# RWKV: the solve by three products on the right-hand side, and values mixed in rows of tokens

## The chip, the cores and the metric

The kernel runs on one core of a Trainium2 chip. The time is the device time of one execution in microseconds (us), from the first to the last instruction on the core. In the text PE is the engine that multiplies matrices (TensorE), DVE the vector engine, ACT the activation engine (ScalarE), POOL the GpSimd engine, and SP the engine that issues nearly all transfers.

## The reference, cut to what matters

The model has two blocks on 256 tokens of width 2048; all is in float32. The change lies in the second block, in a group of 16 RWKV heads of 64 channels. For each token the projection p is mixed with that of the token before it, and a recurrence runs over the tokens:

```
prev = jnp.pad(p, ((0, 0), (1, 0), (0, 0)))[:, :-1]
p = p + (prev - p) * mu
r, k, v, xw, xa, xg = split_cols_2(p, RWKV_SPLITS)
...
def step(state, inp):
    r_t, w_t, k_t, v_t, kk_t, a_t = inp
    sa = jnp.einsum('bhvk,bhk->bhv', state, -kk_t)
    state = (state * w_t[:, :, None, :]
             + sa[..., None] * (kk_t * a_t)[:, :, None, :]
             + v_t[..., None] * k_t[:, :, None, :])
    return state, jnp.einsum('bhvk,bhk->bhv', state, r_t)
```

The kernel doesn't run the recurrence token by token. It takes the tokens in two blocks of 128. Within a block the removed part sa of each token depends on those of the tokens before it, which is a triangular system with a unit diagonal, 128 by 128 for each head: (I - N) x = rhs, with N strictly triangular.

## The kernel before

Each projection is a product in three parts (a high and a low part of each factor: lines 163 to 165). The weights arrive by transfers of 512 KB that SP issues (line 159), ACT rounds them to the high part wh (line 148), and DVE forms the low part wl (lines 151 and 154). PE accumulates in acc.

The 16 heads are worked in two halves of 8 (`rwkv_half`, hf = 0 and 1), and a half in two groups of 4 heads (`heads4`, hg = 0 and 1), which are generators run step by step in turn (`together`). A half begins with the projections of k, r and v (`rwkv_in`). The function `project` calls `evac` for each block of tokens, which scales acc into a tile pn with the tokens on the partitions (line 1226); `shifted` transposes pn, so that channels lie on the partitions and tokens in columns, and `shift` mixes each column with the one before it: one activation and one instruction on DVE for each 128 channels (lines 1210 and 1211). For v (the tile rv) the result is transposed back by `rows` to the tile vn, tokens on the partitions, with 8 transposes and two copies (lines 1367 and 1368).

Then come the decay (pd at line 1280, the scan cs at line 1288), the norm of the keys, whose square root is taken by Newton steps on DVE (lines 1312 to 1319: nv, nt, ni), and the matrices sa of both groups and both token blocks (line 1391). The diagonal blocks of 32 by 32 of all 16 systems of the half are inverted together on DVE (lines 1411 and 1412), transposed to invt and invx (lines 1417 and 1418), and `spread` puts them into block-diagonal matrices of 128 by 128, four heads to an instruction (line 1433).

In `heads4` the inverse of the whole system is then formed by doubling the block size twice (l = 5 and 6): pz is the product of the matrix with the inverse so far, zt keeps the part of the level (line 1453), and pw is added to the inverse wt (line 1458). Between the levels wt is transposed to xt by PE and ACT (lines 1445 and 1447). Then pk is formed from v (line 1462), copied to rhs, and pg is the inverse times rhs (line 1471). For the first block (t = 0) rhs has 64 columns for each head, for the second 128. After that come the scores psr, the outputs py, the state pst and, at the end of the half, the norm of the outputs and a gate (the product pgt).

Each engine carries out its instructions in order. The framework sets that order when the kernel is built: it moves the instructions of an engine against each other by its own estimate of when they can start. Projections that belong to later work (`feed`) are laid between the steps of the attention and of half 0. In half 1's solve hardly any are left.

Of the kernel before, what the change touches and what calls it, by code (L numbers as in the profile page):

```python
# [12 lines left out]
AL = mybir.AluOpType  # L13
# [41 lines left out]
def tile_kernel(ctx: ExitStack, tc: tile.TileContext, I: dict, out: bass.AP):  # L55
# [27 lines left out]
    def tl(tag, shape=None, dt=F, name=None):  # L83
        pool, (n, bufs) = (sb, BASE[tag]) if tag in BASE else (phase[1], phase[2][tag])
        shape = [128, n] if shape is None else shape
        return pool.tile(shape, dt, name=name or tag, tag=tag, bufs=bufs)
# [1116 lines left out]
    G.memset(seg2, 1.0)  # L1203
    G.memset(seg2.rearrange("p (n c) -> p n c", c=128)[:, :, 0:1], 0.0)
    strict = cst[:, C_LT:C_LT + 128]
    upto = cst[:, C_LE:C_LE + 128]
# [13 lines left out]
    def shifted(c0, name, nt, dt_, tr, feed=None, early=0):  # L1220
# [14 lines left out]
        return dst  # L1235

    CDEC = math.exp(-0.5)
    yr = []
# [23 lines left out]
    def rwkv_in(hf, feed):  # L1262
        how = ("f", "xt", bgT) if hf else ("m", "g", lambda nat, q: transpose2(lambda t, kt: nat[t][:, kt * 128:(kt + 1) * 128], q))
        kx = shifted(1024 + hf * 512, "rk", *how, feed=feed, early=0 if hf else 2)
        if hf == 0:
            ranks()
        return kx, shifted(hf * 512, "rr", *how), shifted(2048 + hf * 512, "rv", *how)

    def rwkv_half(hf, kx, rx, vx):
        c8 = slice(hf * 4, hf * 4 + 4)  # L1270
# [90 lines left out]

        vn = tl("g", [128, 2, 512], name="vn")

        def rows(dst, x, t):
            p = pside([128, 4, 128], name="prow")
            for q in range(4):
                PE.transpose(p[:, q], x[:, q, t * 128:(t + 1) * 128], ident)
            S.copy(dst, flat(p))

        for t in range(2):  # L1370
            rows(vn[:, t], vx, t)
        kn = tl("l", name="kn")
# [49 lines left out]
        def heads4(hg):  # L1422
            s0 = None
            for t in range(2):
# [12 lines left out]

                wt = spread(invt, "wt")
                xt = spread(invx, "xt")
                for l in range(5, 7):  # L1440
                    yield
                    if l == 6:
                        px = pside([128, 4, 128], name="px")
                        for i in range(4):
                            PE.transpose(px[:, i], wt[:, i], ident)
                        xt = tl("m", [128, 4, 128], name="xt")
                        S.copy(xt, px)
                        yield
                    pz = pside([128, 4, 128], name="pz")
                    for i in range(4):  # L1450
                        PE.matmul(pz[:, i], nt_(i), xt[:, i], start=True, stop=True)  # L1451
                    zt = tl("m", [128, 4, 128], name="zt")
                    V.tensor_tensor(zt, pz, bc4(lev[:, l * 128:(l + 1) * 128]), op=AL.mult)
                    yield
                    pw = pside([128, 4, 128], name="pw")
                    for i in range(4):
                        PE.matmul(pw[:, i], zt[:, i], wt[:, i], start=True, stop=True)  # L1457
                    V.tensor_tensor(wt, pw, wt, op=AL.add)
                yield
# [6 lines left out]
                if t:  # L1466
                    G.tensor_copy(rhs[:, :, 64:], an[:, hv].rearrange("p (h k) -> p h k", h=4))
                yield
                pg = pside([128, 4, 128], name="pg")
                for i in range(4):  # L1470
                    PE.matmul(pg[:, i, :n], wt[:, i], rhs[:, i, :n], start=True, stop=True)
                ga = tl("m", [128, 4, 128], name="ga")
# [440 lines left out]
```

## Time and profile before

| | us |
|---|---|
| three runs | 2555.61, 2565.97, 2565.65 (median 2565.65) |
| profiled execution, its own time | 2557.92 |
| its span in the trace | 2556.2 |
| PE busy | 2422.8 (95%) |
| DVE busy | 1796.2 (70%) |
| ACT busy | 1170.2 (46%) |
| POOL busy | 172.1 (7%) |

The times of the three runs and of the profiled execution differ by 10 us. Starts in the trace are counted from the beginning of the span. In a timeline row the figure in brackets is how long the engine stood idle before the instruction, and what ended it. An f32 product shows as two instructions of PE, so a row of 8 heads reads x16. The granted clock of PE was 0.984 of full speed over the span.

### The profile page before, as it was taken

Reading aid. Unit: us, or ns where it says so; the run is one execution under the profiler, and the core shown is the slowest. Engines: PE = TensorE matmul, PEld = TensorE weight load, DVE = VectorE, ACT = ScalarE, POOL = GpSimd, SP = SyncE. Lnnn points to the kernel's source line nnn. Section 1 sums busy time; section 2 is a strip of 40 time slices with the busy share of each in tenths; the row PEclk is TensorE's granted clock in tenths of the full one; section 3 lists DMA queues with packets and bytes.
Section 4 is the critical chain, followed back from the end, with each engine's and each line's share of the span. In section 5 each row is a group of like instructions: output and inputs, shape, how many; then the busy total and the mean of one; then the engine's idle time right before and its main releaser. Section 6 shows DMA issues by size and latency. Waiting matters only on the chain.

```text
span 2556.2 us, 32427 instructions
## 1 busy us (share of the span) xinstructions
PE 2422.8 (95%) x11491; PEld 1928.6 (75%) x11491; DVE 1796.2 (70%) x2991; ACT 1170.2 (46%) x1560; POOL 172.1 (7%) x169
## 2 busy tenths in 40 slices
PE   8999998889989998998999999999999999999998
PEld 5667766778767776787878677787888888888886
DVE  5898657997897888967687978755655544555544
ACT  6543244444653544445642452445544433444433
POOL 0000010220230010002020120100000000000000
PEclk9999999999999999999999999999999999999999
DMA  7877547676656788755633243145466555666554
GB/s 262 276 251 225 170 153 242 218 232 228 198 183 218 233 282 288 259 182 158 198 94 110 80 136 99 63 163 192 133 189 182 186 187 187 189 184 187 201 188 154
DMA packets 267358, 483.11 MB, mean 189 GB/s; under 512 B 21137, under 2 KB 45547, under 8 KB 267195
## 3 DMA queue, kind: packets, MB, share of 16 engines
q1 hardware_dynamic: 266875, 480.60, 58.4%
q8 instruction: 90, 1.47, 0.2%
q14 instruction: 73, 0.60, 0.1%
q10 hardware_dynamic: 320, 0.44, 0.1%
HBM read 477.82 MB, written 3.15 MB: 188 GB/s over the span
## 4 chain that ended last, share of the span: by engine, by line
PE 61%; DVE 18%; DMA 11%; issue 6%; ACT 3%; POOL 1%; SPq 0%; DVEq 0%; ACTq 0%; POOLq 0%
PE acc L165 17%; PE acc L164 17%; PE acc L163 17%; DMA ar<-in_w_ada 8%; DVE wl L154 6%; DVE aa L405 3%; PE trp L236 2%; ACT wh L148 1%; DMA lnb<-in_ln_b 1%; PE pw L1457 1%; PE pz L1451 1%; DVE u L1411 1%; DVE inv L1412 1%; DMA wr<-in_w_in_e 1%; DMA wr<-in_w_in_o 0%
## 5 line engine op out<-in xcount | busy, mean ns | idle before, releaser
L148 ACT CAST wh<-wr 128x1024 fp32r<-128x1024 f32 (+2 forms) x736 | 760.3, 1038 | 991.6 <-PE acc L165 804.6
L164 PE MATMUL acc<-wl,xh 128*128 128x512 f32 (+2 forms) x2560 | 1005.5, 393 | 22.9 <-DVE wl L154 22.7
L163 PE MATMUL acc<-wh,xh 128*128 128x512 f32 (+2 forms) x2560 | 1011.8, 396 | 14.1 <-ACT xh L253 6.1
L165 PE MATMUL acc<-wh,xl 128*128 128x512 f32 (+2 forms) x2560 | 1003.5, 393 | 2.4 <-DVE xl L254 1.9
L154 DVE TENSOR_TENSOR wl<-wr,wh 128x512 fp32r<-128x512 f32 (+2 forms) x928 | 622.3, 702 | 176.8 <-ACT wh L148 176.1
L164 PEld LDWEIGHTS acc<-wl,xh 128*128 128x128 f32 x2560 | 485.1, 189 | 135.8 <-DVE wl L154 37.2
L151 DVE TENSOR_TENSOR wl<-wr,wh 128x1024 fp32r<-128x1024 f32 x272 | 333.3, 1225 | 357.4 <-ACT wh L148 355.4
L163 PEld LDWEIGHTS acc<-wh,xh 128*128 128x128 f32 x2560 | 484.6, 189 | 127.1 <-ACT wh L148 10.0
L165 PEld LDWEIGHTS acc<-wh,xl 128*128 128x128 f32 x2560 | 484.8, 189 | 106.3 <-issue 4.0
L405 DVE SCALAR_TENSOR_TENSOR aa<-ar,cs,aa 128x512 f32<-128x512 f32 x240 | 191.0, 796 | 72.8 <-DMA ar<-in_w_ada 71.5
L165 PE MATMUL acc<-wh,ucl 128*128 128x512 f32 x128 | 50.9, 398 | 0.0
L164 PE MATMUL acc<-wl,uch 128*128 128x512 f32 x128 | 50.7, 396 | 0.0
L163 PE MATMUL acc<-wh,uch 128*128 128x512 f32 x128 | 49.8, 389 | 0.0
L381 DVE SCALAR_TENSOR_TENSOR am<-ar,cs,am 128x512 f32<-128x512 f32 x60 | 42.6, 746 | 7.3 <-DMA ar<-in_w_ada 7.3
L722 PE MATMUL pp<-eq,ek 128*128 128x128 f32 x224 | 29.4, 286 | 6.1 <-DVE ek L734 6.1
L722 PEld LDWEIGHTS pp<-eq,ek 128*128 128x128 f32 x224 | 28.5, 201 | 8.4 <-issue 5.0
L1055 POOL TENSOR_TENSOR sgo<-sgo,psc 128x512 f32<-128x512 f32 x8 | 14.6, 1850 | 295.5 <-ACT sgo L1049 164.8
L350 PE MATMUL ada<-wl,c 128*4 128x512 f32 x64 | 26.0, 406 | 4.2 <-DVE wl L154 4.2
L164 PE MATMUL acc<-wl,dh 128*128 128x512 f32 x64 | 26.2, 410 | 3.8 <-DVE wl L154 3.7
L457 DVE SCALAR_TENSOR_TENSOR xl<-trp,pr,xh 128x256 fp32r<-128x256 f32 x48 | 22.3, 480 | 10.1 <-ACT xh L456 9.9
L1866 ACT ACTIVATE un<-acc,rml 128x512 f32<-128x512 f32 x32 | 22.0, 689 | 15.6 <-PE acc L165 15.6
L163 PEld LDWEIGHTS acc<-wh,uch 128*128 128x128 f32 x128 | 24.4, 191 | 5.6
(592 smaller groups left out, 2457.3 us busy)
## 6 DMA issues: line engine op xcount, KB each, us to landing
ar<-in_w_ada SPq DMA_DIRECT2D x288, 256.0 KB
wr<-in_w_in_e SPq DMA_DIRECT2D x128, 512.0 KB
wr<-in_w_up SPq DMA_DIRECT2D x128, 512.0 KB
wr<-in_w_down SPq DMA_DIRECT2D x128, 512.0 KB
wr<-in_w_in SPq DMA_DIRECT2D x80, 512.0 KB
wr<-in_w_in_o SPq DMA_DIRECT2D x64, 512.0 KB
wr<-in_w_ada SPq DMA_DIRECT2D x64, 256.0 KB
wr<-in_w_out_e SPq DMA_DIRECT2D x32, 512.0 KB
```

The lines of the kernel that those rows point to most:

```text
L148: S.copy(wh, wr)
L151: engines[0].tensor_tensor(wl, wr, wh.bitcast(F), op=AL.subtract)
L154: engines[q % 2].tensor_tensor(wl[:, q], wr[:, q], wh[:, q].bitcast(F), op=AL.subtract)
L163: PE.matmul(acc, xh, wh, start=start, stop=False)
L164: PE.matmul(acc, xh, wl, start=False, stop=False)
L165: PE.matmul(acc, xl, wh, start=False, stop=stop)
L236: PE.transpose(pt[:, q, t * 128:(t + 1) * 128], src(t, kt + q), ident)
L350: PE.matmul(acc, c4[:, k0 + q], wl[:, q], start=False, stop=k0 + q == 15)
L381: V.scalar_tensor_tensor(acc[a], w[:, q], col, acc[a], op0=AL.mult, op1=AL.add)
L405: V.scalar_tensor_tensor(acc, w, cs[:, k:k + 1], acc, op0=AL.mult, op1=AL.add)
L722: PE.matmul(pp[:, h, t], kx[:, 2 * h + c, s * 128:(s + 1) * 128], qx[:, 2 * h + c, t * 128:(t + 1) * 128], start=c == 0, stop=c == 1)
L1411: V.tensor_tensor(u, inv[:, j + 1:, j:j + 1].to_broadcast([128, n, j]), inv[:, j:j + 1, :j].to_broadcast([128, n, j]), op=AL.mult)
```

## The change

There are two edits. First, v is no longer transposed, mixed in columns and transposed back. A new function, `shifted_rows`, leaves v in rows of tokens: ACT scales acc into pn as before, a transfer issued from ACT's queue copies the rows 0 to 126 of pn into the rows 1 to 127 of a second tile pv, another brings the last row of the first block into the first row of the second, and for the first block the first row is cleared by POOL. The mixing constants arrive as a broadcast (mur, 512 columns). DVE then forms vn in three instructions for each block of tokens: pv - pn, times mur, plus pn.

Second, the inverse of the 128 by 128 system is not formed. With D the block-diagonal inverse (spread to dt and dx) and M the part of the product of N with D outside the diagonal blocks (pmm, masked by the new constant off32 into mt), the solution is D times a sum of powers of M on rhs. There are four diagonal blocks, so the sum ends with the third power: x = rhs, then three times x = M x + rhs (px, and x on DVE), and pg is D times x.

```
--- before.py
+++ after.py
@@ -1202,6 +1202,8 @@
     seg2 = tl("c", name="seg2")
     G.memset(seg2, 1.0)
     G.memset(seg2.rearrange("p (n c) -> p n c", c=128)[:, :, 0:1], 0.0)
+    off32 = pconst([128, 128], "off32")
+    V.tensor_scalar(off32, cst[:, C_BD32:C_BD32 + 128], -1.0, 1.0, op0=AL.mult, op1=AL.add)
     strict = cst[:, C_LT:C_LT + 128]
     upto = cst[:, C_LE:C_LE + 128]
     bc4 = lambda m: m[:, None, :].to_broadcast([128, 4, 128])
@@ -1232,6 +1234,29 @@
             for r in range(2):
                 k = c0 // 128 + q + r
                 shift(dst[:, q + r], pt[:, r], pr3[:, MU + k:MU + k + 1], omu[:, k:k + 1])
+        return dst
+
+    def shifted_rows(c0, name, nt, dt_):
+
+        nat, prev = {}, {}
+        mu = bcast("bc", I["rwkv_mu_2"][0, c0:c0 + 512], 512, name="mur")
+
+        def evac(cb, t, acc):
+            nat[t] = tl(nt, name="pn")
+            prev[t] = tl(nt, name="pv")
+            S.activation(nat[t], acc, AF.Identity, scale=rs1[t])
+            nc.scalar.dma_start(prev[t][1:], nat[t][:127])
+            if t:
+                nc.scalar.dma_start(prev[t][:1], nat[0][127:])
+            else:
+                G.memset(prev[t][:1], 0.0)
+
+        project(hT, w2, c0, 512, evac, lead=0)
+        dst = tl(dt_, [128, 2, 512], name=name)
+        for t in range(2):
+            V.tensor_tensor(prev[t], prev[t], nat[t], op=AL.subtract)
+            V.tensor_tensor(prev[t], prev[t], mu, op=AL.mult)
+            V.tensor_tensor(dst[:, t], prev[t], nat[t], op=AL.add)
         return dst
 
     CDEC = math.exp(-0.5)
@@ -1264,9 +1289,9 @@
         kx = shifted(1024 + hf * 512, "rk", *how, feed=feed, early=0 if hf else 2)
         if hf == 0:
             ranks()
-        return kx, shifted(hf * 512, "rr", *how), shifted(2048 + hf * 512, "rv", *how)
-
-    def rwkv_half(hf, kx, rx, vx):
+        return kx, shifted(hf * 512, "rr", *how), shifted_rows(2048 + hf * 512, "vn", *how[:2])
+
+    def rwkv_half(hf, kx, rx, vn):
         c8 = slice(hf * 4, hf * 4 + 4)
         wup = tl("m", name="wup")
         nc.sync.dma_start(wup[:64], I["w_decay_up_2"][0][:, hf * 512:(hf + 1) * 512])
@@ -1359,16 +1384,12 @@
             S.activation(e, e, AF.Exp, scale=-CDEC)
             V.scalar_tensor_tensor(flat(kk[:, qs]), flat(kk[:, qs]), -1.0, flat(e), op0=AL.mult, op1=AL.mult)
 
-        vn = tl("g", [128, 2, 512], name="vn")
-
         def rows(dst, x, t):
             p = pside([128, 4, 128], name="prow")
             for q in range(4):
                 PE.transpose(p[:, q], x[:, q, t * 128:(t + 1) * 128], ident)
             S.copy(dst, flat(p))
 
-        for t in range(2):
-            rows(vn[:, t], vx, t)
         kn = tl("l", name="kn")
         rows(kn, kx, 0)
         bn = tl("l", name="bn")
@@ -1435,27 +1456,13 @@
                     return d
 
 
-                wt = spread(invt, "wt")
-                xt = spread(invx, "xt")
-                for l in range(5, 7):
-                    yield
-                    if l == 6:
-                        px = pside([128, 4, 128], name="px")
-                        for i in range(4):
-                            PE.transpose(px[:, i], wt[:, i], ident)
-                        xt = tl("m", [128, 4, 128], name="xt")
-                        S.copy(xt, px)
-                        yield
-                    pz = pside([128, 4, 128], name="pz")
-                    for i in range(4):
-                        PE.matmul(pz[:, i], nt_(i), xt[:, i], start=True, stop=True)
-                    zt = tl("m", [128, 4, 128], name="zt")
-                    V.tensor_tensor(zt, pz, bc4(lev[:, l * 128:(l + 1) * 128]), op=AL.mult)
-                    yield
-                    pw = pside([128, 4, 128], name="pw")
-                    for i in range(4):
-                        PE.matmul(pw[:, i], zt[:, i], wt[:, i], start=True, stop=True)
-                    V.tensor_tensor(wt, pw, wt, op=AL.add)
+                dt = spread(invt, "dt")
+                dx = spread(invx, "dx")
+                pm = pside([128, 4, 128], name="pmm")
+                for i in range(4):
+                    PE.matmul(pm[:, i], dx[:, i], nt_(i), start=True, stop=True)
+                mt = tl("m", [128, 4, 128], name="mt")
+                V.tensor_tensor(mt, pm, bc4(off32), op=AL.mult)
                 yield
                 pk = pside([128, 4, 64], name="pk")
                 for i in range(4):
@@ -1465,10 +1472,18 @@
                 n = 128 if t else 64
                 if t:
                     G.tensor_copy(rhs[:, :, 64:], an[:, hv].rearrange("p (h k) -> p h k", h=4))
+                x = rhs
+                for _ in range(3):
+                    yield
+                    px = pside([128, 4, 128], name="px")
+                    for i in range(4):
+                        PE.matmul(px[:, i, :n], mt[:, i], x[:, i, :n], start=True, stop=True)
+                    x = tl("m", [128, 4, 128], name="x")
+                    V.tensor_tensor(x[:, :, :n], px[:, :, :n], rhs[:, :, :n], op=AL.add)
                 yield
                 pg = pside([128, 4, 128], name="pg")
                 for i in range(4):
-                    PE.matmul(pg[:, i, :n], wt[:, i], rhs[:, i, :n], start=True, stop=True)
+                    PE.matmul(pg[:, i, :n], dt[:, i], x[:, i, :n], start=True, stop=True)
                 ga = tl("m", [128, 4, 128], name="ga")
                 S.copy(ga[:, :, :n], pg[:, :, :n])
                 yield
```

The change moves instructions on the engines. Three places are shown, each as the engine's order lists it (line, operation, output and inputs; "waits" are the semaphores of other engines or transfers, and a row with x2 stands for two instructions in succession).

On DVE at the end of the v projection of half 0, before, with the waits (rv is v mixed in columns, cs the scan of the decay):

```order
L154 TENSOR_TENSOR wl<-wr,wh 128x512 [waits DMAHW3_49,Activation_49]
L154 TENSOR_TENSOR wl<-wr,wh 128x512
L154 TENSOR_TENSOR wl<-wr,wh 128x512 [waits DMAHW4_49,PE_49,Activation_49]
L1211 SCALAR_TENSOR_TENSOR rv<-trp,pr_2763,rv 128x255 [waits Activation_49] x2
L154 TENSOR_TENSOR wl<-wr,wh 128x512
L1211 SCALAR_TENSOR_TENSOR rv<-trp,pr_2763,rv 128x255 [waits Activation_49] x2
L154 TENSOR_TENSOR wl<-wr,wh 128x512 [waits DMAHW5_49,DVE_49,Activation_49]
L154 TENSOR_TENSOR wl<-wr,wh 128x512
L1288 SCALAR_TENSOR_TENSOR cs<-seg_9821,sgm 128x512 [waits Activation_49] x2
```


The same place after (pv is the shifted copy, vn the mixed values):

```order
L154 TENSOR_TENSOR wl<-wr,wh 128x512
L1257 TENSOR_TENSOR pv<-pv,pn 128x512 [waits DMAHW7_49,Activation_49,Pool_49]
L1258 TENSOR_TENSOR pv<-pv,mur 128x512 [waits DVE_49]
L1259 TENSOR_TENSOR vn<-pv,pn 128x512 [waits DVE_49]
L154 TENSOR_TENSOR wl<-wr,wh 128x512 [waits DMAHW4_49,PE_49,Activation_49]
L1257 TENSOR_TENSOR pv<-pv,pn 128x512 [waits DMAHW2_49,DMAHW1_49]
L154 TENSOR_TENSOR wl<-wr,wh 128x512
L1258 TENSOR_TENSOR pv<-pv,mur 128x512 [waits DVE_49]
L154 TENSOR_TENSOR wl<-wr,wh 128x512 [waits DMAHW5_49,Activation_49]
L1259 TENSOR_TENSOR vn<-pv,pn 128x512 [waits DVE_49]
L1313 SCALAR_TENSOR_TENSOR cs<-seg_9821,sgm 128x512 [waits Activation_49] x2
```


The instruction that waits for the transfer, pv with DMAHW7, stands ahead of a wl that was free of V's work, and the second one ahead of the next wl.

On DVE at the end of the v projection of half 1, before (nv, nt and ni are the Newton steps of the key norm, fa a factor of the keys):

```order
L154 TENSOR_TENSOR wl<-wr,wh 128x512 x15
L1211 SCALAR_TENSOR_TENSOR rv<-pbg,pr_2763,rv 128x255 x2
L154 TENSOR_TENSOR wl<-wr,wh 128x512
L1312 TENSOR_SCALAR nv<-pn 8x256
L1313 TENSOR_SCALAR nt<-nv 8x256
L1332 TENSOR_SCALAR fa<-av,pr_2763,oka 128x256
L1211 SCALAR_TENSOR_TENSOR rv<-pbg,pr_2763,rv 128x255 x2
L1314 TENSOR_SCALAR ni<-nt 8x256
L1315 TENSOR_SCALAR nv<-nv 8x256
```


And after:

```order
L154 TENSOR_TENSOR wl<-wr,wh 128x512 x14
L1337 TENSOR_SCALAR nv<-pn 8x256
L1257 TENSOR_TENSOR pv<-pv,pn 128x512
L1338 TENSOR_SCALAR nt<-nv 8x256
L1258 TENSOR_TENSOR pv<-pv,mur 128x512
L1339 TENSOR_SCALAR ni<-nt 8x256
L1259 TENSOR_TENSOR vn<-pv,pn 128x512
L1257 TENSOR_TENSOR pv<-pv,pn 128x512
L1340 TENSOR_SCALAR nv<-nv 8x256
L1258 TENSOR_TENSOR pv<-pv,mur 128x512
L1342 TENSOR_TENSOR nt<-ni 8x256
L1259 TENSOR_TENSOR vn<-pv,pn 128x512
```


The mixing of v is woven into the Newton steps, and the two splits wl that stood ahead of nv, apart from the long run, have gone behind it.

On DVE in the solve of half 1, first block of tokens, before (zt and wt are the two instructions of a level; sr is the masked score):

```order
L1433 TENSOR_TENSOR wt<-invt,cst 128x512
L1433 TENSOR_TENSOR xt<-invx,cst 128x512
L1433 TENSOR_TENSOR wt<-invt,cst 128x512
L1433 TENSOR_TENSOR xt<-invx,cst 128x512
L1453 TENSOR_TENSOR zt<-pz,lev 128x512 x2
L1458 TENSOR_TENSOR wt<-pw,wt 128x512 x2
L1453 TENSOR_TENSOR zt<-pz,lev 128x512 x2
L1458 TENSOR_TENSOR wt<-pw,wt 128x512 x2
L1464 COPY rhs<-pk 128x4x64 x2
L1391 TENSOR_TENSOR sr<-psr,cst 128x512 x4
```


And after (dt and dx are the spread inverses, mt the masked product, x the three steps):

```order
L1454 TENSOR_TENSOR dt<-invt,cst 128x512
L1454 TENSOR_TENSOR dx<-invx,cst 128x512
L154 TENSOR_TENSOR wl<-wr,wh 128x512 x2
L1465 TENSOR_TENSOR mt<-pmm,off_9824 128x512
L1454 TENSOR_TENSOR dt<-invt,cst 128x512
L1454 TENSOR_TENSOR dx<-invx,cst 128x512
L1465 TENSOR_TENSOR mt<-pmm,off_9824 128x512
L1471 COPY rhs<-pk 128x4x64 x2
L1482 TENSOR_TENSOR x<-px,rhs 128x4x64 x6
L1412 TENSOR_TENSOR sr<-psr,cst 128x512 x4
```


Before, the four spreads stood in succession; now those of the second group of heads stand behind mt of the first, which waits for PE.

## Rows read from the trace of the kernel before

**Rows 1.** The page: busy time by engine, then the chain by line.

```profile
PE 2422.8 (95%) x11491; PEld 1928.6 (75%) x11491; DVE 1796.2 (70%) x2991; ACT 1170.2 (46%) x1560; POOL 172.1 (7%) x169
...
PE acc L165 17%; PE acc L164 17%; PE acc L163 17%; DMA ar<-in_w_ada 8%; DVE wl L154 6%; DVE aa L405 3%; PE trp L236 2%; ACT wh L148 1%; DMA lnb<-in_ln_b 1%; PE pw L1457 1%; PE pz L1451 1%; DVE u L1411 1%; DVE inv L1412 1%; DMA wr<-in_w_in_e 1%; DMA wr<-in_w_in_o 0%
```

**Rows 2.** Busy us of PE, PEld, DVE, ACT, POOL; PE clock, DMA share, GB/s.

```profile
1280.00:1300.00 20.00, 19.33 (x88) 13.67 (x87) 16.13 (x37) 12.69 (x22) 1.36 (x1) 1.00 0.35 108
...
1440.00:1460.00 20.00, 18.21 (x87) 13.49 (x86) 19.07 (x69) 11.12 (x20) 1.11 (x3) 1.00 0.17 53
...
1580.00:1600.00 20.00, 19.44 (x193) 18.37 (x192) 13.39 (x20) 5.13 (x14) 0.64 (x1) 1.00 0.00 1
```

**Rows 3.** DVE's groups by line and shape from 1080 to 1660 us.

```profile
L1453 DVE TENSOR_TENSOR zt<-pz,lev 128x512 f32<-128x512 f32 x16 | 11.0, 690 | 9.9 <-PE pz L1451 9.9
...
L1433 DVE TENSOR_TENSOR xt<-invx,cst 128x512 f32<-128x512 f32 x8 | 8.3, 1036 | 0.0
...
L1464 DVE COPY rhs<-pk 128x256 f32<-128x256 f32 x8 | 3.4, 425 | 2.5 <-PE pk L1462 1.9
...
L1211 DVE SCALAR_TENSOR_TENSOR rv<-trp,pr,rv 128x255 f32<-128x255 f32 x4 | 1.7, 476 | 0.0
```

**Rows 4.** The tile prow: count, duration min/median/max in ns, first and last start.

```profile
L1367 PE MATMUL prow<-cst,rv x16: 272/272/332, 1310.4 to 1519.5; 128*128 128x128 f32 x16
```

**Rows 5.** Timeline, end of V in half 0: start, us, engine, idle before.

```profile
1278.12 0.69 ACT L1226 ACTIVATE pn<-acc,rmix 128x512 f32<-128x512 f32 x1 [0.26 <-PE acc L165]
...
1280.23 0.87 PE L236 MATMUL trp<-cst,pn 128*128 128x128 f32 x6
...
1280.29 0.58 SPq L1273 DMA_DIRECT2D wup<-in_a_up  x1
...
1281.14 0.69 DVE L154 TENSOR_TENSOR wl<-wr,wh 128x512 fp32r<-128x512 f32 x1 [1.96 <-ACT wh L148]
...
1281.88 0.40 PE L164 MATMUL acc<-wl,xh 128*128 128x512 f32 x1
...
1283.62 3.15 PE L1280 MATMUL pd<-lora,wup 64*128 64x256 f32 x16 [0.21 <-DMA wup<-in_w_decay_up]
```

**Rows 6.** Timeline: a broadcast of 256 KB issued, and its reader.

```profile
1200.73 0.33 SPq L139 DMA_DIRECT2D lng<-in_ln_g  x1
...
1204.12 3.00 POOL L1145 TENSOR_TENSOR z<-z,lng 128x512 f32<-128x512 f32 x2 [3.42 <-DMA lng<-in_ln_g]
```

**Rows 7.** Timeline: a transfer's issue on ScalarE's queue.

```profile
0.80 0.41 ACTq L135 DMA_DIRECT2D cst<-in_cst  x1
```

**Rows 8.** Timeline, end of V in half 1.

```profile
1496.44 0.69 ACT L1226 ACTIVATE pn<-acc,rmix 128x512 f32<-128x512 f32 x1 [0.26 <-PE acc L165]
...
1501.71 0.41 DVE L1312 TENSOR_SCALAR nv<-pn 8x256 f32<-8x256 f32 x1 [0.17 <-PE pn L1308]
...
1504.98 1.40 DVE L1319 SCALAR_TENSOR_TENSOR ni<-nt,ni 8x256 f32<-8x256 f32 x1
```

**Rows 9.** Timeline, the solve of half 1, tokens 0 to 127.

```profile
1573.99 3.91 PE L1451 MATMUL pz<-xt,sa 128*128 128x128 f32 x16 [4.89 <-DVE xt L1433]
...
1579.91 0.66 PE L1445 MATMUL px<-cst,wt 128*128 128x128 f32 x4
...
1585.13 1.90 PE L1462 MATMUL pk<-vn,sa 128*128 128x64 f32 x16
...
1586.87 1.95 PE L1471 MATMUL pg<-rhs,wt 128*128 128x64 f32 x16
...
1588.74 0.71 PE L1389 MATMUL psr<-rr,av 64*128 64x128 f32 x8
```

**Rows 10.** Timeline, the solve of half 1, tokens 128 to 255.

```profile
1595.66 0.37 ACT L1494 COPY y<-py 128x256 f32<-128x256 f32 x1 [1.36 <-PE py L1490]
...
1608.03 2.00 PE L1471 MATMUL pg<-rhs,wt 128*128 128x128 f32 x16
...
1609.97 0.72 PE L1389 MATMUL psr<-rr,av 64*128 64x128 f32 x8
```

## The prediction

> **What bounds the kernel now.** I read the page first: TensorE (PE) is busy 95% of the span, and on the chain that ended last the two products of the inverse, pz and pw, hold 1% each [rows 1]. A share of the whole span says little about one stage, so I cut the stretch of the RWKV halves into pieces of 20 us. The reader is to see there three different limits: at the end of the V projection of half 0 PE is busy 19.33 of 20 us, since projection products fill its gaps; in the stretch of the top-k DVE is, with 19.07 against PE's 18.21; and in the solve of half 1 PE is again, 19.44 against 13.39, but on small products that wait for each other, with hardly a projection product left to put between them [rows 2]. So work that leaves PE in half 0 is worth something only as far as what comes later is limited by PE, and in half 1 the order of a chain of short steps decides. Then I read single lines for prices [rows 3, 4], and the timeline where V ends and where the solve runs.
>
> **What goes, in work.** Per half V loses 8 transposes in and 8 out, (the latter are 16 instructions over both halves, [rows 4]), 4 activations and two copies on ScalarE, and 4 mixing instructions of 0.476 us on DVE [rows 3]. It gains six DVE instructions over 128x512; a 128x512 product of two operands on DVE took 0.690 [rows 3], so 6 x 0.69 = 4.1 come for 4 x 0.48 = 1.9: DVE has 2.2 us more. In the solve DVE loses, for each of the two blocks of tokens, 4 zt and 4 wt of 0.690 (5.5 us) and gains 2 mt of 0.69 and 6 x; at 64 columns an x is like rhs, 0.425 [rows 3], so 3.9 us (1.6 less), at 128 columns 5.5 us (no change). On PE a block had four steps of 8 products (pz and pw at two levels), 8 transposes px of 1.3 us together [rows 9], pk and pg; now it has one step pmm, pk, three px and pg. A step of 8 products takes, from start to start, 1.74 at 64 columns (pk to pg) and 1.94 at 128 (pg to psr) [rows 9, 10]: the columns hardly count. So 4 x 1.94 + 1.3 + 2 x 1.74 = 12.5 becomes 1.94 + 5 x 1.74 = 10.6 where the right-hand side has 64 columns, and 12.7 becomes 1.74 + 5 x 1.94 = 11.4 where it has 128. Six transposes of V took 0.87 on the way in [rows 5], so the 16 are worth some 2 us, and PE loses about 1.9 + 1.3 + 2 = 5 us per half. That sum is not the answer: it is paid only where PE waits for nothing.
>
> **V in half 0.** The pn tile of the first block is there at 1278.12 + 0.69 = 1278.81 [rows 5]. ScalarE then issues the transfer (an issue on its queue took 0.41, [rows 7]) and it lands. No transfer between two tiles on the chip is in this trace. The nearest row by size is the broadcast of 256 KB, issued at 1200.73 + 0.33, for which GpSimd waited until 1204.12: 3.06 us [rows 6]. The nearest by place is the 128 KB of a_up, whose issue ended at 1280.87 and whose reader ran at 1283.62 after waiting 0.21: at most 2.75 [rows 5]. From below, nothing in the trace excludes a landing so quick that nobody waits. I take 3.1, since 127 rows of 2 KB are 254 KB. The subtraction then starts at 1278.81 + 0.41 + 3.1 = 1282.3. The order on DVE decides what this costs: the fifteenth split of a weight (wl) now stands behind three V instructions, the first of which waits for the transfer. It ran at 1281.14 [rows 5]; now it ends at 1282.3 + 4 x 0.69 = 1285.1, and the product that reads it (1281.88 before, [rows 5]) and two behind it, 0.7 us together, stand ahead of the decay product pd on PE. So pd starts at 1285.1 + 0.7 = 1285.8, against 1283.62: **+2.2 us**. If the transfer lands in time, the V instructions fit in the 1.96 us that DVE idled before that wl, and pd is earlier by the transposes that are gone: -1.1. The transfer's landing is thus a range of -1.1 to +2.2 at the head of the chain pd, decay, scan, inverse; each further microsecond adds one.
>
> The Trainium skill, "DMA: Bandwidth & Descriptors", section "Rules for kernel authors", says to issue a transfer early and wait for it late, since its fixed cost hides only behind work. Here the wait comes right behind the issue, and the queue behind the waiting instruction holds the weights for PE, so the rule speaks against this edit; the same page gives about 2.0 us of fixed cost (section "Anatomy of one DMA", measured for transfers issued by GpSimd), and by that, with 254 KB at the page's 436 GB/s, an estimate of 2.6 us would make the term +1.7. The trace agrees in kind: 3.06 us for 256 KB [rows 6].
>
> **V in half 1.** The norm product no longer stands behind the transposes, so the Newton chain's first instruction (nv, 1501.71, [rows 8]) can start 1.9 us earlier, at 1499.8. But the V instructions are woven into that chain, and pn of the first block is ready at 1496.44 + 0.69 = 1497.13 [rows 8], so with the same 3.5 us pv arrives at 1500.6. From there the order has six V instructions of 0.69 and, between them and up to the long Newton instruction ni, six small ones of 0.41 at most, like nv [rows 8], at an estimated 0.35 each: 1500.6 + 4.1 + 2.1 = 1506.8 against 1504.98, 1.8 later. Two splits fewer, 1.4 us, stand before the normalised key, and one more, 0.7, between it and the inverse: 1.8 - 1.4 + 0.7 = **+1.1 us** at the start of the inverse, on an engine that idles little there.
>
> **The solve.** In half 1, block 0, the first product on PE starts at 1573.99 as before and has its half of 3.91 us [rows 9], to 1575.95. Before, all four spreads of the block-diagonal inverse had run by then, back to back. Now the second pair stands behind the first group's mt: 0.1 + 0.69, then two spreads of 1.036 [rows 3], then half a step (0.97) on PE: 1579.8. From there five steps of 1.74 lead to psr at 1588.5, against 1588.74: **-0.2**. Block 1: the copy of y ends at 1595.66 + 0.37 [rows 10]; then ymean and y (1.5 with their small step), mt 0.69, two spreads 2.1, half a step 1.0: 1601.3; pk 1.74, three px and pg of 1.94 lead to 1610.8, against 1609.97: **+0.8**. In half 1 that is +0.6. In half 0 projection products run between the steps, and the order has 27 more of them ahead of that half's end; at 0.23 us from one to the next (the three of one split in 0.7, as above) 6.2 us of PE, and with them 9 splits, 6.2 us of DVE, are done early. They would pay in the top-k stretch, where DVE is the limit [rows 2]; but the two scans of half 1, 2.3 us, now lie there too, and only some four splits (2.8) are gone from it. I set this at nothing, and give the late second pair the same +0.6. The two broadcasts of mu are issued by SP long ahead of their use, and what ScalarE no longer copies was not waited for outside the px transposes counted above.
>
> **Sum.** Half 0: 2.2 + 0.6; half 1: 1.1 + 0.6; after the end of half 1 the order on PE and DVE is that of before. Together +4.5 us on the profiled run's 2557.9: 2562.4. That run lies below the median of the three shown (2565.65) and above their lowest (2555.61); the four together centre on 2561.8, to which the sum gives 2566.3. I predict 2565 us: no change that a measurement of this kernel can tell, which is 0.5%, or 12.8 us.
>
> **Rivals.** (a) *PE's work decides.* If PE is the limit all along, as its 95% suggests [rows 1], both halves' 5 us and nothing of the waits shows: -10, 2552 around the centre. For it: full slices in half 0 and the solve of half 1 [rows 2]. Against it: DVE's 19.07 in between, and the solve's start in half 1 is a chain, not a heap of work. Chance 0.25, and about half of it passes the bound of 0.5%. (b) *The transfer holds DVE up.* Each of four waits (two blocks, two halves) stands at the head of DVE's queue. If landing takes 6 us rather than 3.1, because the packets queue behind 512 KB weight tiles that SP keeps issuing, the first of each half adds 2.9 to the two V terms, and the second, issued behind it, as much again where DVE has caught up: 4 x 2.9 = 12 more, 2578, slower by about the bound. It decides from a landing of 2 us on, where the 1.96 us of idle time are used up [rows 5]. For it: GpSimd waited 3.42 us of a broadcast's landing [rows 6]. Against it: the DMA share at this place is 0.35 of the 16 engines [rows 2]. Chance 0.2. (c) *Contention between DVE and GpSimd.* The new V instructions read two tiles on the chip while GpSimd forms rk and e. If each stretches by half a microsecond, 12 x 0.5 = 6 more, 2571; nothing in the rows shows it, chance 0.05. (d) *The early products pay.* If the top-k stretch loses the 9 splits in full, its limit, DVE, ends 6.2 us sooner; with the +4.5 that makes -1.7, 2560. For it: DVE's 19.07 of 20 there [rows 2]. Against it: the scans that moved in. Chance 0.2. The forecast itself keeps 0.3.
>
> The chances by cases: faster by over 0.5%: half of (a), 0.12, and a tail of (d), 0.14 together; slower: most of (b) and the tail of the forecast, 0.17; within: 0.69. The range reaches from (a) at 2552, a little further since the early products can come on top of it, to (b): 2549 to 2579; the forecast's own, by the bounds of the transfer, is 2558 to 2571.
>
> **What would show it.** DVE idling before the subtraction of pv with the transfer as releaser, some 2 to 3 us in half 0, and pd about 2 us later behind the last projection product: right. If that idle is under 0.5 us the V term is wrong. In the solve of half 1 the second dt must start after the first mt, and psr must lie 15.5 to 17 us behind the end of invx in block 0. The steps px must follow each other at 1.7 to 2.0 us; at 2.5 or more the chain through x binds and the terms are too small. A time under 2550 would mean that PE's work was paid in full.

## The result and the profile after

The changed kernel takes 2620.9 us (median of 6 runs, 2606 to 2632) against 2559.8 before (6 runs): 1.0237 times as long, with a 95% interval of 1.0214 to 1.0260. That is 61 us slower, where 5 were forecast, and outside the range.

The page of the changed kernel, busy time and the group of the first V instruction (busy us, mean ns of one | idle time of its engine just before, and what ended it):

```profile
PE 2450.5 (93%) x11427; PEld 1951.3 (74%) x11427; DVE 1793.8 (68%) x2996; ACT 1158.1 (44%) x1538; POOL 171.3 (7%) x171
...
L1257 DVE TENSOR_TENSOR pv<-pv,pn 128x512 f32<-128x512 f32 x4 | 2.8, 693 | 44.3 <-DMA pv<-pn 44.3
```

DVE's work is what it was [rows 1]. The line to see is the second: four instructions of 0.69 us, and 44.3 us of idle time ahead of them, all ended by the transfer. The stretches, to be read against [rows 2] (busy us of PE, PEld, DVE, ACT, POOL; PE clock, DMA share, GB/s):

```profile
1280.00:1300.00 20.00, 11.35 (x36) 7.02 (x34) 2.68 (x4) 7.36 (x12) 0.00 (x0) 0.67 0.15 53
...
1540.00:1560.00 20.00, 7.25 (x16) 4.55 (x17) 12.09 (x23) 1.15 (x2) 6.50 (x5) 0.50 0.15 47
...
1620.00:1640.00 20.00, 19.34 (x86) 18.36 (x86) 6.71 (x13) 0.00 (x0) 0.00 (x0) 0.50 0.09 27
```

At the end of V in half 0 PE was busy 19.33 of 20 us and is now 11.35, at a granted clock of 0.67. The same place in half 1 has 7.25. The third line is another matter: here PE is busy 19.34 of 20 us, in the solve of half 1, and all the while at a clock of 0.50, which is 1.2 GHz. Two causes, then, and each has its rows.

The timeline of the changed kernel at the end of V in half 0, to [rows 5]:

```profile
1277.38 1.20 ACTq L1248 DMA_DIRECT2D pv<-pn  x1
...
1278.65 5.68 ACTq L1250 DMA_DIRECT2D pv<-pn  x1
...
1284.37 0.65 ACTq L1248 DMA_DIRECT2D pv<-pn  x1
...
1285.24 2.48 PE L1305 MATMUL pd<-lora,wup 64*128 64x256 f32 x12 [2.95 <-DMA wup<-in_w_decay_up]
...
1285.11 1.99 ACT L148 CAST wh<-wr 128x1024 fp32r<-128x1024 f32 x2 [5.80 <-issue]
...
1293.43 0.69 DVE L1257 TENSOR_TENSOR pv<-pv,pn 128x512 f32<-128x512 f32 x1 [15.70 <-DMA pv<-pn]
...
1304.00 0.69 DVE L1257 TENSOR_TENSOR pv<-pv,pn 128x512 f32<-128x512 f32 x1 [7.83 <-DMA pv<-pn]
...
1305.35 0.80 PE L164 MATMUL acc<-wl,xh 128*128 128x512 f32 x1 [7.47 <-DVE wl L154]
...
1307.02 2.33 DVE L1313 TENSOR_TENSOR_SCAN cs<-seg,sgm 128x512 f32<-128x512 f32 x2
```

And the scan of the decay in the kernel before:

```profile
1285.63 2.34 DVE L1288 TENSOR_TENSOR_SCAN cs<-seg,sgm 128x512 f32<-128x512 f32 x2
```

The first transfer is issued by 1278.58 and its reader starts at 1293.43: 14.9 us where the prediction took 3.1. The second reader waits another 7.83 us. ACT is caught too: its second issue takes 5.68 us, and the rounding of the weights behind it starts at 1285.11. pd starts 8.6 us behind the first pn (1276.66), 3 us later than before (5.5), and it waits there for its own weights wup and not for a split: the product that reads the split behind the first wait stands behind pd, at 1296.23, and the next one stands until 1305, 7.47 us of it at a stretch. The chain is held one step further on. The scan cs stands on DVE behind both waits and starts 30.4 us behind pn, where it started 7.5 behind it before. What the transfer does meanwhile, in the transfers of a stretch in half 1 in which nearly nothing else moves (GB/s in 40 slices, the packets, then the share of the time of 16 engines that ACT's queue took):

```profile
GB/s 28 27 23 27 27 23 27 23 27 23 27 23 23 27 23 23 28 23 27 23 23 27 23 23 27 23 27 23 23 27 23 27 23 23 27 23 23 27 23 27
...
DMA packets 225, 0.45 MB, mean 25 GB/s; under 512 B 7, under 2 KB 7, under 8 KB 225
...
q10 hardware_dynamic: 225, 0.45, 6.6%
```

Alone on the queues it moves 25 GB/s, evenly, less than a quarter of what the queues moved on average over the stretch of before [rows 2]. Its packets took 6.6% of the time of 16 engines; one engine busy all the time would be 6.3%. 254 KB at 25 GB/s are 10 us, and two such transfers one behind the other 20. In half 0 the two readers started 14.9 and 25.4 us behind the first issue; the difference is not taken apart here. In half 1, to [rows 8]:

```profile
1523.31 0.41 DVE L1337 TENSOR_SCALAR nv<-pn 8x256 f32<-8x256 f32 x1 [2.12 <-PE pn L1333]
...
1536.15 0.69 DVE L1257 TENSOR_TENSOR pv<-pv,pn 128x512 f32<-128x512 f32 x1 [12.42 <-DMA pv<-pn]
...
1546.75 0.69 DVE L1257 TENSOR_TENSOR pv<-pv,pn 128x512 f32<-128x512 f32 x1 [8.32 <-DMA pv<-pn]
...
1551.48 0.79 PE L164 MATMUL acc<-wl,xh 128*128 128x512 f32 x1 [21.68 <-DVE wl L154]
```

The Newton chain did start earlier (nv 3.2 us behind the pn of v, before 5.3), and then stood for two landings.

The solve of half 1, to [rows 9, 10]:

```profile
1618.96 2.05 PE L1463 MATMUL pmm<-sa,dx 128*128 128x128 f32 x8 [4.94 <-DVE dx L1454]
...
1623.80 2.04 PE L1463 MATMUL pmm<-sa,dx 128*128 128x128 f32 x8 [0.66 <-DVE dx L1454]
...
1625.64 3.52 PE L1469 MATMUL pk<-vn,sa 128*128 128x64 f32 x16
...
1628.94 3.62 PE L1480 MATMUL px<-rhs,mt 128*128 128x64 f32 x16
...
1632.36 7.04 PE L1480 MATMUL px<-x,mt 128*128 128x64 f32 x32
...
1639.18 3.62 PE L1486 MATMUL pg<-x,dt 128*128 128x64 f32 x16
...
1642.73 1.23 PE L1410 MATMUL psr<-rr,av 64*128 64x128 f32 x8
...
1667.58 4.63 PE L1480 MATMUL px<-x,mt 128*128 128x128 f32 x32
...
1674.08 0.72 PE L1410 MATMUL psr<-rr,av 64*128 64x128 f32 x8
```

A step of 8 products takes 3.3 to 3.4 us from start to start (pk to px, px to px) where 1.74 was counted. From the first product to psr are 23.8 us in place of 14.75, and from there to psr of the second block 31.4 in place of 21.2.

In the two profiles the loss of 65 us lies in three stretches: 25 from V's first pn in half 0 to the one in half 1, 21 from there to the first product of half 1's solve, and 19 from that product to the gate.

### The profile page after: what moved, and what is told of

It is laid out like the page before. It is cut to its first block, busy times and chain, and to the rows that moved or that the text cites. A ratio compares the mean times of both kernels' runs of the same rounds, so it can differ in the third digit from the quotient of the medians.

```text
span 2621.2 us, 32290 instructions
## 1 busy us (share of the span) xinstructions
PE 2450.5 (93%) x11427; PEld 1951.3 (74%) x11427; DVE 1793.8 (68%) x2996; ACT 1158.1 (44%) x1538; POOL 171.3 (7%) x171
## 4 chain that ended last, share of the span: by engine, by line
PE 62%; DVE 16%; DMA 11%; issue 6%; ACT 3%; POOL 1%; ACTq 1%; SPq 0%; DVEq 0%; POOLq 0%
PE acc L165 17%; PE acc L164 17%; PE acc L163 17%; DMA ar<-in_w_ada 6%; DVE wl L154 4%; DVE aa L405 3%; PE trp L236 2%; DMA pv<-pn 1%; ACT wh L148 1%; PE px L1480 1%; DMA lnb<-in_ln_b 1%; DMA wr<-in_w_kv_cross 1%; DMA wr<-in_w_in_o 0%; PE psr L1410 0%; PE pmm L1463 0%
## 5 line engine op out<-in xcount | busy, mean ns | idle before, releaser
L1257 DVE TENSOR_TENSOR pv<-pv,pn 128x512 f32<-128x512 f32 x4 | 2.8, 693 | 44.3 <-DMA pv<-pn 44.3
```

## The experiments

Ratios are to the kernel before, timed on the same chip, with 95% intervals. All single edits to the kernel before have "only" in their description.

**Each half of the change alone, and the copy cut.** Four runs: the change with

```
-            nc.scalar.dma_start(prev[t][1:], nat[t][:127])
+            nc.scalar.dma_start(prev[t][1:113], nat[t][:112])
+            nc.scalar.dma_start(prev[t][113:], nat[t][112:127])
```

> The changed kernel with the copy of 127 rows of pn cut into two, 112 rows and 15 rows. Theory 'few engines': the trace of the changed kernel shows 254 KB moving at some 25 GB/s, a sixteenth of what larger transfers reach, so the 127 rows lie on one of the 16 DMA engines; with 112 rows (a multiple of 16) and 15 they spread, each pair lands within 4 us of its issue, the waits of DVE before the subtraction of pv fall from 44.3 us to under 12, and the kernel gets 35 to 45 us faster than the changed one (about 2575 to 2585). Rival 'queue': the transfer is slow because ACT's queue or the weight tiles of 512 KB hold it up; then two pieces in place of one change nothing, the waits stay over 35 us and the time near 2620. Theory 'solve clock' adds that the solve of half 1 still runs at half the granted clock here.

the solve alone (heads4 as changed, `shifted` and `rows` for v as before):

> The kernel before with only the solve changed (M on the right-hand side, values mixed as before). Theory 'solve clock': in the changed kernel the solve of half 1 runs at a granted clock of 0.50 for some 40 us, and the gap that the second pair of spreads leaves on PE behind the idle time of the inverse is what keeps it low; it has nothing to do with V, so the same is seen here, with steps of 8 products at 3.4 us, and the kernel is 12 to 22 us slower than before (2572 to 2582). Rival 'aftermath': the low clock follows from the long idle times in V some 60 us earlier; then the clock is back to 1.00 within 6 us of the first product as before, and the kernel takes 2555 to 2565.

the values alone (`shifted_rows` as changed, heads4 as before):

> The kernel before with only the values changed (rows of tokens, copy of 127 rows as in the changed kernel; inverse formed as before). Theory 'few engines' with 'solve clock' apart: the waits for pv stay at 40 to 48 us, and the kernel is 38 to 48 us slower than before (2598 to 2608). Rival 'aftermath': the whole loss comes with V, 2610 to 2625, and the solve of half 1 runs at half clock here too.

and the values alone with the cut copy:

> Only the values changed, and the copy cut into 112 and 15 rows. Theory 'few engines': waits for pv under 12 us in all, and the kernel within 0.4% of before (2555 to 2570), about +2 us by the terms of the prediction for V. Rival 'queue': as slow as with 127 rows in one piece, 2595 or more.

| | median us | ratio (95%) |
|---|---|---|
| whole change, copy cut | 2576.2 | 1.0073 (1.0047 to 1.0098) |
| only the solve | 2571.3 | 1.0053 (1.0032 to 1.0073) |
| only the values, 127 rows | 2606.3 | 1.0186 (1.0152 to 1.0220) |
| only the values, copy cut | 2565.3 | 1.0024 (1.0011 to 1.0036) |

The parts add up: 0.0186 + 0.0053 = 0.0239, and the whole is 0.0237. Cutting the copy takes 41 us out of the values (1.0186 to 1.0024) and leaves the bytes as they were. The waits, first the line of the values alone with 127 rows, then with the copy cut (us in total, times, longest):

```profile
DVE pv L1257 <- DMA pv<-pn: 44.3, 4, 15.8
```

```profile
DVE pv L1258 <- DMA pv<-pn: 7.0, 2, 5.5
...
ACT wh L148 <- issue: 7.1, 4, 2.5
```

The second of these lines, ACT's idle time before a rounding that no wait explains, is no mark of the copy: before the change it is 8.2.

The rival 'queue' falls, and so does 'aftermath': the solve alone runs slow, and its clock stays at 0.50 with PE busy in full, with nothing wrong in V (windows of the solve alone, columns as above):

```profile
1572.00:1576.00 4.00, 4.00 (x20) 4.00 (x21) 1.11 (x2) 0.00 (x0) 0.00 (x0) 0.50 0.00 0
...
1600.00:1604.00 4.00, 4.00 (x30) 3.77 (x30) 0.86 (x2) 0.51 (x2) 0.55 (x2) 0.50 0.02 4
...
1608.00:1612.00 4.00, 3.50 (x31) 3.53 (x32) 1.90 (x4) 0.25 (x1) 0.00 (x0) 1.00 0.00 0
```

**Is it the number of pieces, or the count of rows?**

```
-            nc.scalar.dma_start(prev[t][1:113], nat[t][:112])
-            nc.scalar.dma_start(prev[t][113:], nat[t][112:127])
+            nc.scalar.dma_start(prev[t][1:114], nat[t][:113])
+            nc.scalar.dma_start(prev[t][114:], nat[t][113:127])
```

> Only the values changed, copy cut into 113 and 14 rows in place of 112 and 15. Theory 'few engines' as the count of rows sets it: 113, like 127, has no divisor up to 16 but 1, so this piece of 226 KB again lies on one engine, and at 25 GB/s takes 9 us: waits for pv of 34 to 42 us in all, kernel 2592 to 2604. Rival 'two pieces': any cut halves the trouble, waits about 7 us as with 112 and 15, kernel about 2565.

It took 2599.4 us (two runs), 1.0160 (1.0114 to 1.0207), and the wait is back:

```profile
DVE pv L1258 <- DMA pv<-pn: 39.9, 4, 14.9
```

One row moved from a piece to the other costs 33 us of waiting: the count of rows decides, not the pieces. The Trainium skill states the rule in "DMA: Bandwidth & Descriptors", section "Why a DMA increments its semaphore by 16 and not by 1": a transfer issued by SP or ACT uses the largest number of engines up to 16 that divides the outermost dimension on both sides, and it gives 127 partitions as an example that ends on one engine. The runs agree: 25 GB/s and one sixteenth of the engines' time for 127 rows, waits of 39.9 us for 113, and 7.0 for 112 with 15.

**What keeps the clock down in the solve?** Only the solve, with more work in the first block of tokens:

```
+                else:
+                    G.memset(rhs[:, :, 64:], 0.0)
+                w = 128
...
-                        PE.matmul(px[:, i, :n], mt[:, i], x[:, i, :n], start=True, stop=True)
+                        PE.matmul(px[:, i, :w], mt[:, i], x[:, i, :w], start=True, stop=True)
```

(x and pg likewise).

> Only the solve changed, and in the first block of tokens the products px and pg made over 128 columns in place of 64 (the upper half of rhs is cleared): more work on PE, the same result. In the run with only the solve changed PE was busy 4.00 of every 4 us and still stayed at a granted clock of 0.50 for 36 us, as long as the products had 64 columns, and came back in the second block, where they have 128; before, pz and pw with 128 columns came back after about 6 us. Theory 'narrow products': with 128 columns the clock is back at 1.00 within 10 us of the first product, steps px take 2 us rather than 3.5, and the kernel is 8 to 14 us faster than with 64 columns (2557 to 2564). Rival 'gap': the idle time between the two groups' pmm holds the clock down; then padding changes nothing or costs up to 2 us (2570 to 2575).

And with 64 columns, but all four spreads first:

```
                 dx = spread(invx, "dx")
+                yield
```

> Only the solve changed, 64 columns, but the four spreads run first, back to back, as before, so that the second group's pmm follows the first's without a gap. Theory 'narrow products': the clock still stays at 0.50 through the first block of half 1; gain 1 to 3 us from the shorter chain (2567 to 2571). Rival 'gap': the clock is back within 6 us, and the kernel is 10 to 15 us faster than with the late spreads (2556 to 2562).

With 128 columns: 2561.4 us, 1.0017 (0.9998 to 1.0036), where 64 gave 1.0053: some 9 us less, on twice the columns, though the two intervals just touch. With the spreads first: 2570.3, 1.0046 (1.0025 to 1.0068), no gain that can be told. PE's steps of the first block with 128 columns:

```profile
1587.06 3.73 PE L1464 MATMUL px<-rhs,mt 128*128 128x128 f32 x16
...
1590.58 4.15 PE L1464 MATMUL px<-x,mt 128*128 128x128 f32 x32
...
1594.57 2.10 PE L1470 MATMUL pg<-x,dt 128*128 128x128 f32 x16
```

The clock comes back during the second px step (two steps in 4.15 us), and not with the spreads first and 64 columns, though PE has no gap there any more:

```profile
1592.00:1596.00 4.00, 4.00 (x21) 4.00 (x20) 0.85 (x2) 0.00 (x0) 0.00 (x0) 0.50 0.02 4
...
1612.00:1616.00 4.00, 4.00 (x21) 4.00 (x21) 4.00 (x5) 0.37 (x1) 0.00 (x0) 0.50 0.00 0
```

So the rival 'gap' falls for the first block: the clock stayed low without it. Both edits together, only the solve:

> Only the solve changed, with 128 columns in the first block and the four spreads first. With 128 columns alone 2561, 0.17% over before. By the prediction's terms the spreads in front take 0.8 us off three or four blocks: 2557 to 2561; if the idle time behind the inverse with them in front is shorter and the clock comes back earlier, 2552 to 2557.

2555.1 us, 1.0006 (0.9988 to 1.0024): as before the change, and with its interval apart from that of the same kernel with 64 columns (1.0046). So with the solve alone the width is worth some 10 us. From the first product to psr its profile has 14.0 us (1571.70 to 1585.67), against 14.75 before.

That the wide products bring the clock back is not shown, though. Here are pk with both edits, and the clock at the same place with the spreads first and 64 columns:

```profile
1575.42 2.60 PE L1451 MATMUL pk<-vn,sa 128*128 128x64 f32 x16
...
1588.00:1592.00 4.00, 4.00 (x20) 4.00 (x21) 1.81 (x3) 0.00 (x0) 0.00 (x0) 0.50 0.00 0
```

Up to pk the products of the two kernels are the same: pk has 64 columns in both, and the first widened product, px, comes only at 1577.86. With both edits the clock came back within pk (2.60 us for its 8 products, where 3.52 is the time at 0.50); with 64 columns it did not. In all four profiles with 64 columns (the whole change, with the copy cut, and the solve alone with late and early spreads) the clock stayed at 0.50 through the first block. In all six with 128 columns it was back within 14 us of the first product, but in four of the six before a widened product had run. There is one profile of each kernel, so what decides when the clock comes back, and by what way the width gains its time, stays open.

**The rest of V.** With the copy cut, the values still cost 0.24%. First with the mixing issued later in the program (the six DVE instructions behind the norm products of the keys):

> Only the values changed, copy cut into 112 and 15 rows, and the three instructions on DVE for each block of tokens issued later in the program (behind the norm products of the keys). With the copy cut, DVE still waited 7.0 us for it and the kernel took 2565, 0.24% over before. Theory 'waiting': these 7 us are the rest of the loss, and with other work ahead of the wait they are gone: within 0.1% of before (2555 to 2561). Rival 'work': the rest is the 2.2 us more on DVE per half and ACT's issues (4.1 us in half 0); then 2563 to 2567 as without.

2571.3 us, 1.0057 (1.0038 to 1.0075): a miss, slower than without. The order of half 1 had hardly changed, and in half 0 DVE stood as long, now for ACT's rounding of the weights:

```profile
1291.98 0.69 DVE L1260 TENSOR_TENSOR pv<-pv,pn 128x512 f32<-128x512 f32 x1 [5.26 <-ACT wh L148]
```

Why it is slower still, and not the same, is open; in its profile V begins 3 us later than with the copy cut alone, in a part that neither edit touches. Then without any transfer, in a kernel that leaves out the mixing with the token before:

> Only the values changed, and the transfers left out: the difference to the token before is replaced by pn - pn, so the mixing with the previous token is not computed, while DVE keeps its six instructions of 128x512 a half. Theory 'waiting': with no transfer and no issues on ACT the kernel is at or below before (2548 to 2558), since PE loses 2 us of transposes per half. Rival 'work': DVE's larger instructions alone cost 4 to 8 us, 2562 to 2567.

2557.7 us, 1.0004 (0.9989 to 1.0020): DVE's larger instructions, with PE's transposes saved, cost nothing that can be told, so the rest is transfer or issue. ACT's queue was held by issues for 4.1 us in half 0. So the same transfers from SP's queue:

```
-            nc.scalar.dma_start(prev[t][1:113], nat[t][:112])
+            nc.sync.dma_start(prev[t][1:113], nat[t][:112])
```

(all three).

> Only the values changed, 112 and 15 rows, but the transfers issued from SP's queue instead of ACT's. Theory 'issue': the rest of V's loss comes from ACT, which issues for some 4 us in half 0 before it rounds the next weights; then ACT's idle time with 'issue' goes, and the kernel is within 0.1% of before (2555 to 2560). Rival 'landing': the wait on DVE stays as long, 2562 to 2567; slower still if the weights behind them on SP's queue come late.

2560.4 us, 0.9997 (0.9976 to 1.0019), and no wait for pv is left. The interval overlaps that of ACT's queue (1.0011 to 1.0036) a little. Its first transfer and the reader, then ACT's idle time before its roundings:

```profile
1276.86 0.62 SPq L1248 DMA_DIRECT2D pv<-pn  x1
...
1277.52 0.90 SPq L1249 DMA_DIRECT2D pv<-pn  x1
...
1280.38 0.68 DVE L1258 TENSOR_TENSOR pv<-pv,pn 128x512 f32<-128x512 f32 x1
...
ACT wh L148 <- issue: 11.9, 6, 3.2
```

From the first issue to the reader are 3.5 us, without idle time on DVE: at most the price that the prediction had meant to pay (0.41 + 3.1). On ACT's queue the same two pieces had taken 5.9 us, of which DVE waited 5.5. So the queue matters, but the theory 'issue' is not shown: its sign did not come, since ACT's idle time with 'issue' is 11.9 us here and was 7.1 on its own queue. What went is the wait on DVE, which the rival 'landing' expected to stay. Whether the 0.24% was ACT's time or the later landing is open.

**All repairs together.**

> The whole change with the copy cut into 112 and 15 rows and 128 columns in the first block of tokens. Theory 'few engines' with 'narrow products': 2576 less some 10, 2562 to 2570, within 0.4% of before. If the two causes were not the whole of it, 2572 or more.

> As the kernel with the copy cut and 128 columns, and the four spreads first besides. By the terms of the prediction (the second pair of spreads late costs 0.8 us in a block of tokens, four blocks): 1 to 4 us faster than without, 2559 to 2568. Rival: the gap alone had kept the clock low, then this is faster by 8 or more.

> Copy cut into 112 and 15 rows, 128 columns in the first block, four spreads first, and V mixed later: all repairs together. By the runs so far (0.1% over before with the first three): if waiting was the rest of V's loss, 2 to 5 us faster than that, 2556 to 2561, and so no slower than before; to beat before clearly it would have to be under 2550.

> The whole change repaired: 112 and 15 rows issued from SP's queue, 128 columns in the first block, spreads first. If the issue on ACT was the rest: 2553 to 2558, no slower than before and perhaps 0.1% faster; if not, as with ACT's queue, about 0.1% over before (2559 to 2565).

| | median us | ratio (95%) |
|---|---|---|
| copy cut, 128 columns | 2573.7 | 1.0054 (1.0031 to 1.0077) |
| and spreads first | 2563.8 | 1.0010 (0.9991 to 1.0029) |
| and mixing later | 2568.4 | 1.0050 (1.0032 to 1.0068) |
| spreads first, transfers from SP | 2555.5 | 0.9988 (0.9968 to 1.0008) |

The first is a miss: it was expected at 2562 to 2570, and can't be told from the change with the copy cut alone (1.0073). The spreads in front, worth nothing that can be told with 64 columns, are worth 0.4% here. In the profile without them (the first row below) the clock fell to 0.50 again in the second block, behind the gap between the two pmm, and with them (the second row) it stayed at 1.00:

```profile
1616.00:1620.00 4.00, 4.00 (x21) 4.00 (x21) 1.28 (x3) 0.00 (x0) 0.00 (x0) 0.50 0.00 0
...
1612.00:1616.00 4.00, 4.00 (x35) 3.84 (x35) 2.35 (x4) 0.53 (x1) 0.00 (x0) 1.00 0.00 0
```

The mixing issued later made it worse here as well, and why stays open. The last row beats the changed kernel by some 64 us (0.9988 against 1.0237 of before) and can't be told from the kernel before.

## Why the prediction was wrong

*The price of the transfer.* This step failed: "I take 3.1, since 127 rows of 2 KB are 254 KB". The size was right and the rate was not. The row that it was taken from [rows 6] was a transfer onto 128 partitions; 127 rows go at 25 GB/s. It measured 14.9 us for the first and 44.3 us of waiting in the four places, where +2.2 in one place was counted. The wait at the head of DVE's queue, ahead of the weights' splits, was the one described; the rival that gave it a larger price, with all four waits, put the landing at 6 us and the loss at 12 more. The values alone lost 48. The path from that wait was wrong as well: "the product that reads it" does not stand ahead of pd but behind it, and what was held was the scan cs on DVE, 23 us later behind pn than before. One row was also misread: the 0.21 us in which pd waited in the kernel before ended with w_decay_up and not with a_up [rows 5], so the 2.75 us are no landing that anything waited for.

*The issue on ACT.* Counted at 0.41 us an issue [rows 7]. Behind the transfer of 127 rows an issue of 2 KB took 5.68 us. Even with the copy cut, issuing took 4.1 us in half 0; with the transfers on SP's queue the last 0.24% of V can't be told any more, but whether the issues or the landing made it is not shown.

*The solve.* Also wrong: "From there five steps of 1.74 lead to psr at 1588.5". The number of steps was right, and the order too: the second dt stood behind the first mt. But 1.74 is the step at full clock, and the solve began, as before, at 0.50 behind the idle time of the inverse [rows 9]. The clock there before the change:

```profile
1572.00:1576.00 4.00, 2.01 (x9) 1.96 (x10) 3.71 (x5) 0.00 (x0) 0.00 (x0) 0.50 0.00 0
1576.00:1580.00 4.00, 4.00 (x26) 3.92 (x26) 2.08 (x3) 0.00 (x0) 0.00 (x0) 0.69 0.02 4
```

Before, pz and pw with 128 columns ran there, and the clock came back within the second of them. With 64 columns it did not come back for the whole first block, and the step measured 3.3 to 3.4 us. The sentence "the columns hardly count" was read from steps at full clock and says nothing of the clock. The +0.6 for half 1 measured as 19 us in the profile of the changed kernel (from the first product to the gate 65.4 us, before 46.3), and the solve by itself as 1.0053 over both halves. The prediction's sign for such steps, "at 2.5 or more the chain through x binds", came for another reason: PE was busy 19.34 of 20 us, at half the clock.

*What held.* DVE's 2.2 us more of work a half cost nothing that can be told (1.0004 without the transfers), and the order on DVE moved as it was read. The late second pair of spreads was guessed at +0.8 in a block; with 64 columns that was lost in the low clock, with 128 it was worth 0.4%, or 10 us, in the whole kernel, more than the 3 us that 0.8 in each of four blocks would make, and the profiles point to the clock behind its gap. In the solve alone with 128 columns its worth can't be told (1.0017 against 1.0006). The rival (a), that PE's saved work would be paid in full, was not borne out: with every repair the kernel is 0.9988 (0.9968 to 1.0008) of before, where its price was 0.996.

## What to carry to other kernels

Price a transfer by how many engines carry it, not by its bytes: look at its outermost count first, cut 127 rows into 112 and 15, and read GB/s where it runs alone. Look at what an engine's queue holds behind a wait or an issue, and put both on the queue with least behind it. When a chain of products is made narrower or rearranged right behind a stretch in which PE idled, read the granted clock there before and after, and don't count its steps at full speed.

## What the runs showed of the hardware

A copy of 127 rows of 2 KB between two tiles moved 25 GB/s; the same bytes as 112 and 15 rows, issued from SP's queue, were there within 3.5 us of the first issue. The issue of a single row of 2 KB on ACT's queue took 5.68 us behind a transfer of 127 rows, and 0.55 behind pieces of 112 and 15. And PE, busy 4.00 of every 4 us, most of it on products of 64 columns, stayed at a granted clock of 0.50 for 32 us (1572 to 1604 with only the solve changed); the same chain with 128 columns was back at 1.00 some 14 us after its first product, and the kernel took some 9 us less on twice the columns. What brings the clock back is not settled by these runs.
